# A fixed program order for ACT and DVE in the experts' blocks of a two-layer decoder trunk, with one call for a split ahead of every weight tile

## The chip, the cores and the metric

The kernel runs on one core of a Trainium2 chip. The metric is the time of one execution in device microseconds; lower is better. Engines are named as in the profile: PE does matrix products (PEld loads their stationary operand), ACT is ScalarE, DVE is VectorE, POOL is GpSimd, and SP here only issues DMAs.

## What is computed

Two decoder layers over 256 tokens of width 1024. Each has a mixer (four groups of heads), a feed-forward part and a gated per-layer embedding. The change touches the feed-forward part of the second layer only, which sends each token to two of eight experts:

```python
def moe_swiglu(x, router, w_gate, w_up, w_down):      # x: 256 x 1024, experts 1024 -> 3584 -> 1024
    logits = (x @ router).astype(jnp.float32)
    top_val, top_idx = lax.top_k(logits, TOP_K)        # 2 of 8
    top_w = jax.nn.softmax(top_val, axis=-1)
    combine = jnp.sum(jax.nn.one_hot(top_idx, N_EXPERTS, dtype=jnp.float32) * top_w[..., None], axis=-2)
    out = jnp.zeros_like(x)
    for e in range(N_EXPERTS):
        out = out + combine[..., e:e + 1].astype(x.dtype) * swiglu(x, w_gate[e], w_up[e], w_down[e])
    return out                                         # swiglu: (silu(x @ wg) * (x @ wu)) @ wd
```

All weights are float32.

## The kernel before

**Weights.** Every weight comes as a tile of 128 x 2048 float32 (1 MB). SP loads it into one of the `raw` buffers (seven in this part), in the order of a list (`plan`). For the matrix products a tile is cut into two parts: ACT copies it into `hi` in a rounded format (float32r), and DVE writes the rest, raw minus hi, into `lo`. There are five `hi` and five `lo` buffers in this part. `pop_split` does this, and `ready` is a list of tiles that were split early:

```python
    def ahead(n, parts=2, keep=False):
        ready.extend([pop_split(parts, keep) for _ in range(n)])
    ...
    def pop_split(parts=2, keep=False):
        if ready:
            return ready.pop(0)
        r = pop()
```

**Experts.** The eight experts are taken as four "large" ones (L, up to 128 tokens each) and four "small" ones (S, up to 64 tokens). Per expert, the hidden width of 3584 goes in seven blocks of 512. A block uses six tiles: two for the gate product (g1, g2), two for the up product (u1, u2) and two for the down product (d1, d2), 336 tiles in all. A large tile takes 12 products of 512 columns, a small one 8. `STEPS` pairs a block of a large expert with a block of a small one and puts the down products of the pair before behind them. A pair has twelve tiles, in this order: Lg1, Sg1, Lg2, (turn of the pair before), Sg2, Lu1, Su1, Lu2, Su2, Ld1, Sd1, Ld2, Sd2.

**Work between the tiles.** After Lg2 ACT takes silu of the gate product out of PSUM (`gate_up`, L1328). After Lu2 DVE multiplies it with the up product (L1331). After Sg2 and after Su2 ACT copies the small expert's products out. `turn` transposes the hidden block on PE: for the large expert 4 transposes, then a copy by ACT and a remainder by DVE; for the small one 8 products of 64 columns, silu by ACT (L1349), a product by DVE (L1350), and a split. After an expert's last block `scatter` copies the sums out of PSUM (two splits), multiplies them on PE with the selection, and adds them to `h` on DVE (L1383, four instructions). `gather` collects the tokens of the next two experts.

**What sets the order.** The framework's scheduler puts the instructions of each engine in an order of its own, as long as it respects the data; the order in which the code is written is only its input. On the chip each engine then takes its instructions in that order.

Of the kernel before, what the change touches and what calls it, by code (L numbers as in the profile page):

```python
# [3 lines left out]

# [1 line left out]

# [77 lines left out]
def decoder_trunk(ctx: ExitStack, tc: tile.TileContext, A, out):  # L84
# [27 lines left out]
    def T(tag, shape, dt=F32, keep=False):  # L112
        count[0] += 1
        name = f"{tag}_{count[0]}"
        if phase and tag + "+" in phase["bufs"] and not keep:
            n = BUFS[tag] + phase["bufs"][tag + "+"]
            turn[tag] = (turn.get(tag, -1) + 1) % n
            if turn[tag] >= BUFS[tag]:
                return phase["pool"].tile(shape, dt, name=name, tag=tag + "+", bufs=n - BUFS[tag])
        if tag in BUFS and (keep or not (phase and tag in phase["bufs"])):  # L120
            return sb.tile(shape, dt, name=name, tag=tag, bufs=BUFS[tag])
        return phase["pool"].tile(shape, dt, name=name, tag=tag, bufs=phase["bufs"][tag])

    def PS(tag, shape, dt=F32):
        count[0] += 1
        return ps.tile(shape, dt, name=f"p{tag}_{count[0]}", tag="p" + tag, bufs=BUFS[tag])

    V, S, G, PE = nc.vector, nc.scalar, nc.gpsimd, nc.tensor

    def f(ap):  # L130
        return ap.bitcast(F32)
# [66 lines left out]
    def split(x, o_hi, o_lo, note=True):  # L198
        a = act_copy(o_hi, x)
        b = V.tensor_tensor(o_lo, x, f(o_hi), op=ALU.subtract)  # L200
        if note:
            latest.update(act=a, dve=b)
        return a, b
# [4 lines left out]
    def ahead(n, parts=2, keep=False):  # L208
        ready.extend([pop_split(parts, keep) for _ in range(n)])
# [48 lines left out]
    def mm(o, l, r, start=True, stop=True):  # L258
        pe(PE.matmul(o, l, r, start=start, stop=stop, skip_group_check=True))  # L259
# [878 lines left out]
    def moe(cn, xh, xl):  # L1138
# [110 lines left out]
        def column(v, vx, kind, n, t):  # L1249
            r = rank_of(kind, n)  # L1250
            return v[:, t, 0:1] if (kind, n) == ("L", 0) else vx[:, t, r:r + 1]

        def gather(*places):

            s = T("S2", [P, 2, 256])
            width, at_ = 0, {}
            for kind, n in places:
                w = P if kind == "L" else 64
                at_[kind] = width
                for t in range(2):  # L1260
                    for c in range(2 if kind == "S" else 1):
                        V.tensor_scalar(s[:, t, width + c * w:width + c * w + w], iota[:, :w],
                                        column(pos, posx, kind, n, t), None, op0=ALU.is_equal)
                width += w
            if places[0] == ("L", 0):
                turned_slots(*places[0], s, 0)
            dst = {}
            for kind, n in places:
                if kind == "L":
                    gx = T("x", [P, 2, NK, P], F32R)  # L1270
                    dst[kind] = gx[:, 0], gx[:, 1]
                else:
                    gx = T("xs", [P, NK, P], F32R)
                    dst[kind] = gx[:, :, :64], gx[:, :, 64:]
                xg[kind, n] = gx
            k = 4 if width <= P else 2
            for q in range(NK // k):
                o = PS("e", [P, k, width])
                for c in range(k):
                    cc = slice((k * q + c) * P, (k * q + c + 1) * P)  # L1280
                    for t in range(2):
                        mm(o[:, c], cn[:, t, cc], s[:, t, :width], t == 0, t == 1)
                for kind, n in places:
                    w = P if kind == "L" else 64
                    split(o[:, :, at_[kind]:at_[kind] + w], *[v[:, k * q:k * q + k] for v in dst[kind]])
            for kind, n in places:
                if (kind, n) != ("L", 0):
                    turned_slots(kind, n, s, at_[kind])

        def turned_slots(kind, n, s, c0):  # L1290
            o = PS("e", [P, 2, P])
            for t in range(2):
                transpose(o[:, t, :], s[:, t, c0:c0 + P])
            st = T("S1", [P, 2, P], F32R)
            act_copy(st, o)
            sel[kind, n] = st
# [36 lines left out]
        def turn(u):  # L1333

            s = hid.pop(u)
            if u[0] == "L":
                pt = PS("e", [P, 4, P])
                for c in range(4):
                    transpose(pt[:, c, :], s[:, c * P:(c + 1) * P])
                hh, hl = T("S2", [P, 4, P], F32R), T("S2", [P, 4, P], F32R)  # L1340
                split(pt, hh, hl)
                hT[u] = hh, hl
            else:
                pt = PS("e", [P, 2, 4, 64])
                for g in range(2):
                    for c in range(4):
                        mm(pt[:, g, c, :], s[g][:, c * P:(c + 1) * P], cf[:, CF["halves"]])
                a = T("S1", [P, 4, 64])
                S.activation(a, pt[:, 0], AF.Silu)  # L1349
                V.tensor_tensor(a, a, pt[:, 1], op=ALU.mult)  # L1350
                hs = T("S2", [P, 4, P], F32R)
                split(a, hs[:, :, :64], hs[:, :, 64:])
                hT[u] = hs

        def down(u, q):
            p, b = u[:2], u[2]
# [14 lines left out]
        def scatter(p):  # L1371
            st = sel.pop(p)
            y = []
            for n in range(2):
                y.append((T("S2", [P, 512], F32R), T("S2", [P, 512], F32R)))
                split(acc[p][n], *y[n])
            for t in range(2):
                for n in range(2):
                    o = PS("e", [P, 512])
                    mm(o, st[:, t, :], y[n][0], True, False)  # L1380
                    mm(o, st[:, t, :], y[n][1], False, True)
                    hs = h[:, t, n * 512:(n + 1) * 512]
                    V.scalar_tensor_tensor(hs, o, column(comb, combx, *p, t), hs, op0=ALU.mult, op1=ALU.add)  # L1383

        full()
        gather(("L", 0))
        ahead(2, 4)
        hold()
        weights()
# [2 lines left out]
        chosen.extend(nc.values_load(order[0:1, r:r + 1], engines=[mybir.EngineType.SP], min_val=1, max_val=R)  # L1392
                      for r in range(R))
        follow(S.preload_act_table_set("silu_and_others"), fence["act"])
        ahead(2)
        for u, t in STEPS:
            if t is None:
                for v in u:
                    turn(v)
                done = dict(latest)  # L1400
            elif t < 4:
                gate_up(u, t)
            else:
                down(u, t - 4)
            if (u, t) == (("L", 0, 0), 3):
                gather(("S", 0))
            if t == 5 and u[0] == "L" and u[2] == 4 and u[1] < 3:
                gather(("L", u[1] + 1), ("S", u[1] + 1))
        fence.update(done)

    def spill(cn, pos, comb, capacities, over):
# [223 lines left out]
```

## Time and profile before

| | us |
|---|---|
| median of 3 runs (1661.75 to 1662.02) | 1661.79 |
| the profiled execution | 1662.77 |
| its span, first to last instruction | 1661.0 |

| busy, share | PE | PEld | DVE | ACT | POOL |
|---|---|---|---|---|---|
| whole span | 95% | 80% | 78% | 65% | 5% |
| 710 to 1605 us | 97% | 77% | 90% | 76% | 0% |

The experts' blocks fill the second row's stretch and a little on either side: the first gate product leaves PSUM at 690.86 us. "Busy" of PE is a modelled figure: in a row of matmuls that follow each other without a gap, each is listed with 390 to 400 ns and starts 0.23 us after the one before. What PE was idle for, and whom it waited for, says more than its share. A releaser that the profile names ("<-") is the one that came last.

### The profile page before, as it was taken

Reading aid. Unit: us, or ns where it says so; the run is one execution under the profiler, and the core shown is the slowest. Engines: PE = TensorE matmul, PEld = TensorE weight load, DVE = VectorE, ACT = ScalarE, POOL = GpSimd, SP = SyncE. Lnnn points to the kernel's source line nnn. Section 1 sums busy time; section 2 is a strip of 40 time slices with the busy share of each in tenths; the row PEclk is TensorE's granted clock in tenths of the full one; section 3 lists DMA queues with packets and bytes.
Section 4 is the critical chain, followed back from the end, with each engine's and each line's share of the span. In section 5 each row is a group of like instructions: output and inputs, shape, how many; then the busy total and the mean of one; then the engine's idle time right before and its main releaser. Section 6 shows DMA issues by size and latency. Waiting matters only on the chain.

```text
span 1661.0 us, 22588 instructions
## 1 busy us (share of the span) xinstructions
PE 1582.1 (95%) x8523; PEld 1321.2 (80%) x8523; DVE 1302.6 (78%) x1470; ACT 1073.6 (65%) x1315; POOL 80.2 (5%) x116
## 2 busy tenths in 40 slices
PE   7998999999999998799999999999999999999998
PEld 7897789999888977677787777787777787777776
DVE  5578655455575786788988998898998989989895
ACT  5555554444455563677777777777687777777773
POOL 0024100000000141000000000000000000000000
PEclk9998999999999999899999999999999999999999
DMA  8431465545444222499999999999999999999990
GB/s 324 173 107 57 161 233 176 205 157 210 143 159 183 97 98 77 166 420 386 385 365 397 372 355 398 403 371 370 355 380 386 388 373 362 371 385 388 399 348 26
DMA packets 65489, 461.26 MB, mean 278 GB/s; under 512 B 7392, under 2 KB 7776, under 8 KB 12128
## 3 DMA queue, kind: packets, MB, share of 16 engines
q1 hardware_dynamic: 64224, 455.02, 71.6%
q10 hardware_dynamic: 1152, 4.76, 0.9%
q8 instruction: 68, 1.11, 0.3%
q14 instruction: 45, 0.37, 0.1%
HBM read 458.70 MB, written 1.05 MB: 277 GB/s over the span
## 4 chain that ended last, share of the span: by engine, by line
PE 32%; DVE 12%; ACT 6%; issue 5%; DMA 3%; ACTq 0%; DVEq 0%; POOLq 0%; POOL 0%
DVE lo L200 10%; ACT hi L134 5%; PE pc L255 5%; PE pc L256 4%; PE pc L1305 4%; PE pc L254 4%; PE pc L1306 4%; PE pe L259 4%; PE pd L255 2%; PE pd L256 2%; PE pd L254 2%; DMA raw<-in_moe_dn_dram 2%; DMA raw<-in_moe_gu_dram 1%; PE pe L271 1%; ACT S L134 1%
## 5 line engine op out<-in xcount | busy, mean ns | idle before, releaser
L200 DVE TENSOR_TENSOR lo<-raw,hi 128x2048 fp32r<-128x2048 f32 (+4 forms) x532 | 958.3, 1844 | 183.3 <-ACT hi L134 182.7
L134 ACT ACTIVATE hi<-raw 128x2048 fp32r<-128x2048 f32 (+4 forms) x532 | 796.4, 1556 | 118.8 <-PE pc L256 84.3
L255 PE MATMUL pc<-lo,x 128*128 128x512 f32 x512 | 207.5, 405 | 16.4 <-DVE lo L200 15.8
L254 PE MATMUL pc<-hi,x 128*128 128x512 f32 x512 | 204.0, 399 | 3.2 <-DVE rank L1233 2.1
L256 PE MATMUL pc<-hi,x 128*128 128x512 f32 x512 | 202.8, 396 | 0.0
L1306 PE MATMUL pc<-lo,xs 128*128 128x512 f32 x448 | 178.7, 399 | 7.6 <-DVE lo L200 7.4
L254 PE MATMUL pd<-x,hi 128*128 128x256 f32 x640 | 181.7, 284 | 0.1
L256 PE MATMUL pd<-x,lo 128*128 128x256 f32 x640 | 181.5, 284 | 0.0
L255 PE MATMUL pd<-x,hi 128*128 128x256 f32 x640 | 180.7, 283 | 0.3 <-DVE x L200 0.3
L1305 PE MATMUL pc<-hi,xs 128*128 128x512 f32 x448 | 177.0, 395 | 1.3 <-DVE S L1331 0.9
L255 PEld LDWEIGHTS pc<-lo,x 128*128 128x128 f32 x512 | 96.5, 188 | 55.8 <-DVE lo L200 35.7
L254 PEld LDWEIGHTS pd<-x,hi 128*128 128x128 f32 x640 | 121.6, 190 | 1.6 <-ACT x L134 0.3
L256 PEld LDWEIGHTS pd<-x,lo 128*128 128x128 f32 x640 | 121.6, 190 | 1.6 <-DVE lo L200 0.2
L255 PEld LDWEIGHTS pd<-x,hi 128*128 128x128 f32 x640 | 121.6, 190 | 1.2 <-DVE x L200 0.5
L254 PEld LDWEIGHTS pc<-hi,x 128*128 128x128 f32 x512 | 96.7, 189 | 25.9 <-issue 2.2
L256 PEld LDWEIGHTS pc<-hi,x 128*128 128x128 f32 x512 | 96.7, 189 | 20.7 <-DVE x L200 0.4
L1306 PEld LDWEIGHTS pc<-lo,xs 128*128 128x128 f32 x448 | 84.2, 188 | 34.9 <-DVE lo L200 17.4
L1305 PEld LDWEIGHTS pc<-hi,xs 128*128 128x128 f32 x448 | 84.1, 188 | 21.3 <-DVE S L1331 1.8
L255 PE MATMUL pd<-lo,S 128*128 128x512 f32 x224 | 91.1, 407 | 5.4 <-DVE lo L200 5.4
L256 PE MATMUL pd<-hi,S 128*128 128x512 f32 x224 | 88.3, 394 | 0.0
L1306 PE MATMUL pc<-lo,S 128*128 128x512 f32 x224 | 82.7, 410 | 0.8 <-DVE lo L200 0.8
L254 PE MATMUL pd<-hi,S 128*128 128x512 f32 x224 | 79.4, 395 | 0.0
(278 smaller groups left out, 2290.7 us busy)
## 6 DMA issues: line engine op xcount, KB each, us to landing
raw<-in_moe_gu_dram SPq DMA_DIRECT2D x224, 1024.0 KB, 7.2
raw<-in_moe_dn_dram SPq DMA_DIRECT2D x112, 1024.0 KB, 7.5
raw<-in_ffn_gu_dram SPq DMA_DIRECT2D x28, 1024.0 KB, 5.0
raw<-in_ffn_dn_dram SPq DMA_DIRECT2D x14, 1024.0 KB, 4.9
raw<-in_win_t_dram SPq DMA_DIRECT2D x16, 848.0 KB, 5.2
raw<-in_win_c_dram SPq DMA_DIRECT2D x12, 1024.0 KB, 6.8
raw<-in_cmp_w_dram SPq DMA_DIRECT2D x8, 1024.0 KB, 5.9
raw<-in_w_out_dram SPq DMA_DIRECT2D x8, 1024.0 KB, 4.9
```

The lines of the kernel that those rows point to most:

```text
L134: return S.activation(o, i, AF.Copy, scale=scale)
L200: b = V.tensor_tensor(o_lo, x, f(o_hi), op=ALU.subtract)
L254: pe(PE.matmul(o, lh, rh, start=start, stop=False))
L255: pe(PE.matmul(o, lh, rl, start=False, stop=False))
L256: pe(PE.matmul(o, ll, rh, start=False, stop=stop))
L259: pe(PE.matmul(o, l, r, start=start, stop=stop, skip_group_check=True))
L271: pe(PE.transpose(o, i, ident[:i.shape[0], :i.shape[0]]))
L1305: pe(PE.matmul(o, lhs, rh, start=start, stop=False))
L1306: pe(PE.matmul(o, lhs, rl, start=False, stop=stop))
```

## The change

ACT and DVE get a wrapper (`Engine`). While `keep(True)` holds, each instruction that goes through it is tied to the one issued before it on the same engine, by an ordering dependency that costs no semaphore: the scheduler can no longer move them against each other. PE, SP and POOL are left to the scheduler. Since every call then passes through the wrapper, all of ACT's and DVE's instructions in these blocks carry its line number, L146.

The loop over `STEPS` calls `ahead(1, 1)` before each tile's products. Ahead of the loop, `ahead(2)` becomes `gather(("S", 0))` and `ahead(1)`. Parts of `gather` (four products each with their copies, and the turned selections), the last two steps of the small expert's `turn`, and the four parts of `scatter` are put into a list `later`; one entry of it is issued after each tile's products.

```diff
+    class Engine:
+        def __init__(self, eng):
+            self.eng, self.kept, self.last = eng, False, None
+        def keep(self, on):
+            self.kept, self.last = on, None
+        def __getattr__(self, name):
+            op = getattr(self.eng, name)
+            if not self.kept:
+                return op
+            def given(*args, **kw):
+                ins = op(*args, **kw)
+                if self.last:
+                    follow(ins, self.last)
+                self.last = ins
+                return ins
+            return given
+
+    V, S = Engine(nc.vector), Engine(nc.scalar)
...
-            for q in range(NK // k):
+            def part(q):
                 o = PS("e", [P, k, width])
...
+            for q in range(NK // k):
+                later.append(partial(part, q))
             for kind, n in places:
                 if (kind, n) != ("L", 0):
-                    turned_slots(kind, n, s, at_[kind])
+                    later.append(partial(turned_slots, kind, n, s, at_[kind]))
...
+            def times():
                 V.tensor_tensor(a, a, pt[:, 1], op=ALU.mult)
+            def parts():
                 hs = T("S2", [P, 4, P], F32R)
                 split(a, hs[:, :, :64], hs[:, :, 64:])
                 hT[u] = hs
+            later[:0] = [times, parts]
...
+            later.extend(partial(part, t, n) for t in range(2) for n in range(2))
+        def some(n=None):
+            while later and n != 0:
+                later.pop(0)()
+                n = n and n - 1
...
         ahead(2, 4)
...
-        ahead(2)
+        gather(("S", 0))
+        ahead(1)
+        V.keep(True)
+        S.keep(True)
         for u, t in STEPS:
             if t is None:
                 for v in u:
                     turn(v)
                 done = dict(latest)
-            elif t < 4:
+                continue
+            ahead(1, 1)
+            if t < 4:
                 gate_up(u, t)
             else:
                 down(u, t - 4)
-            if (u, t) == (("L", 0, 0), 3):
-                gather(("S", 0))
+            some(1)
...
+        V.keep(False)
+        S.keep(False)
+        some()
```

The lists below are the built programs' order, engine by engine. In them `hi_1761_9498` is a weight tile's hi part (the numbers tell tiles apart), `pc_...` is a product in PSUM that comes from the tiles named beside it, `pe_...` a small product in PSUM, `S1_...` and `S2_...` are results in SBUF. All are of one pair in the second large expert.

ACT before, from the split of tile Lg2 (`hi_1762`) on; the gate product of Lg1 and Lg2 is `pc_1753`, that of Sg1 and Sg2 (`hi_1772`) is `pc_1757`:

```order
L134 ACTIVATE hi_1762_9502<-raw_1736_9396 128x2048
L134 ACTIVATE hi_1772_9546<-raw_1739_9410 128x2048
L134 ACTIVATE hi_1777_9563<-raw_1742_9428 128x2048
L1328 ACTIVATE S2_1764_9518<-pc_1753_9466 128x512
L134 ACTIVATE S2_1766_9525<-pe_1765_9520 128x512
L134 ACTIVATE hi_1781_9582<-raw_1754_9467 128x2048
L134 ACTIVATE hi_1784_9596<-raw_1758_9486 128x2048
L134 ACTIVATE hi_1787_9615<-raw_1761_9500 128x2048
L1349 ACTIVATE S1_1769_9538<-pe_1768_9529 128x256
L134 ACTIVATE hi_1791_9631<-raw_1771_9544 128x2048
L134 ACTIVATE S2_1770_9541<-S1_1769_9538 128x4x64
L134 ACTIVATE S2_1774_9558<-pc_1757_9485 128x512
```

ACT after the change, from the split of the same tile (Lg2 is `hi_1761` here, Sg2 `hi_1771`, Lu1 `hi_1775`, Su1 `hi_1780`, Lu2 `hi_1784`, Su2 `hi_1787`, Ld1 `hi_1791`):

```order
L146 ACTIVATE hi_1761_9498<-raw_1736_9396 128x2048
L146 ACTIVATE S2_1763_9514<-pc_1753_9460 128x512
L146 ACTIVATE S2_1766_9525<-pe_1765_9520 128x512
L146 ACTIVATE S1_1769_9538<-pe_1768_9529 128x256
L146 ACTIVATE hi_1771_9542<-raw_1739_9410 128x2048
L146 ACTIVATE S2_1773_9554<-pc_1758_9483 128x512
L146 ACTIVATE hi_1775_9559<-raw_1742_9428 128x2048
L146 ACTIVATE S2_1778_9576<-S1_1769_9538 128x4x64
L146 ACTIVATE hi_1780_9581<-raw_1750_9454 128x2048
L146 ACTIVATE hi_1784_9596<-raw_1755_9477 128x2048
L146 ACTIVATE hi_1787_9615<-raw_1760_9496 128x2048
L146 ACTIVATE S2_1789_9627<-pc_1782_9585 128x512
```

The copies out of PSUM (`<-pc`) stood two to five splits behind the split of the tile that completes the product; now each stands directly behind that split, ahead of the next tile's.

DVE before, the same pair, from the remainder of Sg2 (`lo_9547`) to that of Ld1 (`lo_9632`); L1331 is the large expert's product of gate and up:

```order
L200 TENSOR_TENSOR lo_9547<-raw_9410,hi_9546 128x2048
L200 TENSOR_TENSOR lo_9564<-raw_9428,hi_9563 128x2048
L1383 SCALAR_TENSOR_TENSOR h<-pe_9462,combx,h 128x512
L200 TENSOR_TENSOR S_1767_9526<-pe_9520,S_1766_9525 128x512
L200 TENSOR_TENSOR lo_9583<-raw_9467,hi_9582 128x2048
L200 TENSOR_TENSOR lo_9597<-raw_9486,hi_9596 128x2048
L200 TENSOR_TENSOR lo_9616<-raw_9500,hi_9615 128x2048
L1350 TENSOR_TENSOR S_1769_9538<-S_1769_9538,pe_9529 128x256
L1331 TENSOR_TENSOR S_1764_9518<-S_1764_9518,pc_9560 128x512
L200 TENSOR_TENSOR lo_9632<-raw_9544,hi_9631 128x2048
```

DVE after the change, from the remainder of Sg2 (`lo_9543`) to that of Ld1 (`lo_9632`):

```order
L146 TENSOR_TENSOR lo_9543<-raw_9410,hi_9542 128x2048
L146 TENSOR_TENSOR S_1769_9538<-S_1769_9538,pe_9529 128x256
L146 TENSOR_TENSOR lo_9560<-raw_9428,hi_9559 128x2048
L146 TENSOR_TENSOR S_1778_9576<-S_1769_9538,S_1778_9576 128x4x64
L146 TENSOR_TENSOR lo_9582<-raw_9454,hi_9581 128x2048
L146 TENSOR_TENSOR lo_9597<-raw_9477,hi_9596 128x2048
L146 TENSOR_TENSOR S_1763_9514<-S_1763_9514,pc_9563 128x512
L146 TENSOR_TENSOR lo_9616<-raw_9496,hi_9615 128x2048
L146 TENSOR_TENSOR lo_9632<-raw_9540,hi_9631 128x2048
```

The product with `pc_9563`, which needs all of Lu1's and Lu2's matmuls, moved ahead of the remainder of Su2 (`lo_9616`).

## Rows read from the trace of the kernel before

**Rows 1.** The page's span, and busy us (share) xinstructions by engine

```profile
span 1661.0 us, 22588 instructions
PE 1582.1 (95%) x8523; PEld 1321.2 (80%) x8523; DVE 1302.6 (78%) x1470; ACT 1073.6 (65%) x1315; POOL 80.2 (5%) x116
```

**Rows 2.** Busy time by stretch: from:to, us, PE PEld DVE ACT POOL, PEclk, DMA, GB/s

```profile
710.00:1605.00 895.00, 863.85 (x3948) 685.69 (x3947) 807.27 (x511) 679.59 (x531) 0.00 (x0) 1.00 0.98 381
```

**Rows 3.** Waits, 710 to 1605 us: who waits for whom, us in total, times, longest

```profile
ACT S L1328 <- PE pc L256: 75.6, 26, 4.1
...
PE pc L255 <- DVE lo L200: 15.8, 38, 0.9
```

**Rows 4.** Waits of SP's DMA queue, 710 to 1605 us, same columns

```profile
SPq L186 <- DVE lo L200: 560.9, 268, 5.3
```

**Rows 5.** Groups by line and shape, 700 to 1610 us: busy us, mean ns | idle before

```profile
L200 DVE TENSOR_TENSOR lo<-raw,hi 128x2048 fp32r<-128x2048 f32 x329 | 738.3, 2286 | 61.7 <-ACT hi L134 61.7
L1331 DVE TENSOR_TENSOR S<-S,pc 128x512 f32<-128x512 f32 x28 | 19.2, 687 | 19.1 <-PE pc L256 19.1
...
L1383 DVE SCALAR_TENSOR_TENSOR h<-pe,combx,h 128x512 f32<-128x512 f32 x20 | 14.4, 743 | 0.0
L200 DVE TENSOR_TENSOR S<-S,S 128x256 fp32r<-128x256 f32 x28 | 11.7, 418 | 0.0
...
L200 DVE TENSOR_TENSOR x<-pe,x 128x256 fp32r<-128x256 f32 x12 | 4.8, 417 | 1.9 <-ACT x L134 1.9
...
L134 ACT ACTIVATE hi<-raw 128x2048 fp32r<-128x2048 f32 x329 | 610.3, 1912 | 0.0
L134 ACT ACTIVATE S<-pc 128x512 f32<-128x512 f32 x56 | 33.3, 595 | 36.8 <-PE pc L1306 36.6
...
L1349 ACT ACTIVATE S<-pe 128x256 f32<-128x256 f32 x28 | 10.8, 384 | 55.2 <-PE pe L259 55.2
```

**Rows 6.** ACT in order of time: start us, us, what [idle before <-releaser]

```profile
708.06 0.60 ACT L1328 ACTIVATE S<-pc 128x512 f32<-128x512 f32 x1 [3.41 <-PE pc L256]
...
735.45 0.60 ACT L1328 ACTIVATE S<-pc 128x512 f32<-128x512 f32 x1 [2.19 <-PE pc L256]
...
739.00 7.34 ACT L134 ACTIVATE hi<-raw 128x2048 fp32r<-128x2048 f32 x4
...
767.66 0.60 ACT L1328 ACTIVATE S<-pc 128x512 f32<-128x512 f32 x1 [3.03 <-PE pc L256]
...
1566.47 0.60 ACT L1328 ACTIVATE S<-pc 128x512 f32<-128x512 f32 x1 [3.09 <-PE pc L256]
```

**Rows 7.** DVE in order of time, same columns: six remainders in a row

```profile
755.64 13.30 DVE L200 TENSOR_TENSOR lo<-raw,hi 128x2048 fp32r<-128x2048 f32 x6 [1.38 <-ACT hi L134]
```

**Rows 8.** PE's matmuls in order of time, then ACT's copy of their product

```profile
911.64 0.39 PE L1305 MATMUL pc<-hi,xs 128*128 128x512 f32 x1
911.87 0.39 PE L1306 MATMUL pc<-lo,xs 128*128 128x512 f32 x1
...
912.30 0.60 ACT L134 ACTIVATE S<-pc 128x512 f32<-128x512 f32 x1 [1.63 <-PE pc L1306]
```

**Rows 9.** The chain that ended last: half a small expert's turn on PE

```profile
724.78 0.84 PE pe L259 x8
```

**Rows 10.** Busy time by stretch, columns as in rows 2: PE's clock falls

```profile
149.00:158.00 9.00, 8.53 (x25) 5.85 (x26) 7.47 (x24) 4.72 (x15) 3.03 (x4) 0.50 0.35 117
...
662.00:668.00 6.00, 2.83 (x15) 1.90 (x15) 5.24 (x9) 2.47 (x6) 0.75 (x2) 0.92 0.00 0
668.00:673.00 5.00, 4.44 (x22) 2.83 (x20) 3.79 (x6) 3.27 (x6) 0.00 (x0) 0.50 0.30 105
...
1630.00:1636.00 6.00, 5.55 (x15) 4.44 (x16) 6.00 (x7) 5.82 (x7) 0.00 (x0) 0.50 0.02 4
```

**Rows 11.** PE's matmuls in order of time in the last of these stretches

```profile
1632.22 0.63 PE L255 MATMUL pc<-lo,x 128*128 128x512 f32 x1
1632.64 0.63 PE L256 MATMUL pc<-hi,x 128*128 128x512 f32 x1
```

More of the change, by code (lines that the diff above doesn't have):

```diff
@@ L3 @@
 from contextlib import ExitStack, contextmanager
+from functools import partial
 import numpy as np
@@ L126, in PS @@
         return ps.tile(shape, dt, name=f"p{tag}_{count[0]}", tag="p" + tag, bufs=BUFS[tag])
-    V, S, G, PE = nc.vector, nc.scalar, nc.gpsimd, nc.tensor
+    G, PE = nc.gpsimd, nc.tensor
+    class Engine:
[15 more added lines that the diff above has]
+    V, S = Engine(nc.vector), Engine(nc.scalar)
     def f(ap):
@@ L1285, in gather @@
                     split(o[:, :, at_[kind]:at_[kind] + w], *[v[:, k * q:k * q + k] for v in dst[kind]])
+            for q in range(NK // k):
+                later.append(partial(part, q))
             for kind, n in places:
                 if (kind, n) != ("L", 0):
-                    turned_slots(kind, n, s, at_[kind])
+                    later.append(partial(turned_slots, kind, n, s, at_[kind]))
+        later = []
         def turned_slots(kind, n, s, c0):
@@ L1342, in turn @@
                 hT[u] = hh, hl
[L1343 to L1349, printed above, removed]
+                return
+            pt = PS("e", [P, 2, 4, 64])
+            for g in range(2):
+                for c in range(4):
+                    mm(pt[:, g, c, :], s[g][:, c * P:(c + 1) * P], cf[:, CF["halves"]])
+            a = T("S1", [P, 4, 64])
+            S.activation(a, pt[:, 0], AF.Silu)
+            def times():
                 V.tensor_tensor(a, a, pt[:, 1], op=ALU.mult)
+            def parts():
                 hs = T("S2", [P, 4, P], F32R)
@@ L1376, in scatter, with part @@
                 split(acc[p][n], *y[n])
[L1377 to L1383, printed above, removed]
+            def part(t, n):
+                o = PS("e", [P, 512])
+                mm(o, st[:, t, :], y[n][0], True, False)
+                mm(o, st[:, t, :], y[n][1], False, True)
+                hs = h[:, t, n * 512:(n + 1) * 512]
+                V.scalar_tensor_tensor(hs, o, column(comb, combx, *p, t), hs, op0=ALU.mult, op1=ALU.add)
+            later.extend(partial(part, t, n) for t in range(2) for n in range(2))
[3 more added lines that the diff above has]
+                n = n and n - 1
         full()
         gather(("L", 0))
+        some()
         ahead(2, 4)
@@ L1404, in moe @@
                 down(u, t - 4)
-            if (u, t) == (("L", 0, 0), 3):
-                gather(("S", 0))
+            some(1)
             if t == 5 and u[0] == "L" and u[2] == 4 and u[1] < 3:
                 gather(("L", u[1] + 1), ("S", u[1] + 1))
+        V.keep(False)
+        S.keep(False)
+        some()
         fence.update(done)
```

## The prediction, made before the changed kernel ran

> **What bounds the kernel now.** On the page PE is busy 95% of the span and DVE 78% [rows 1], an average over stages, so I read the table by stretch next, then the waits there, then the groups by line, then two engines in order of time. In the experts' part PE is busy 863.85 of 895 us at the full clock [rows 2], so 31.2 us of idle time is all that a better order of the splits can win. PE waits, when it does, for `lo`, the last step of a split [rows 3]. ACT waits much longer for PE: 75.6 us in 26 waits before silu of the gate product alone [rows 3]. That costs nothing, because ACT has by then split the tiles that PE needs next: the copy stands two to five splits behind its tile in the order printed above. DVE is the next engine: 807 of 895 us [rows 2], 738.3 us of its time being remainders [rows 5]. SP issues its loads when DVE has freed a raw buffer [rows 4], so transfers follow DVE and set nothing. A pair of twelve tiles takes 767.66 - 735.45 = 32.21 us where no gather or scatter falls in it, and (1566.47 - 708.06) / 26 = 33.02 us in the mean of 26 [rows 6].
>
> **What the change does to the lead.** `pop_split` hands out from `ready` as long as something is in it. When the loop starts, `ready` holds two tiles; `ahead(1)` takes the first and puts it back at the end, the first `ahead(1, 1)` turns the list back, and two products later it is empty. From the third tile on, `ahead(1, 1)` splits the very tile whose products follow. So in program order a split stands directly ahead of its own products, behind everything that the tile before gave to ACT and DVE, and the wrapper makes that order binding. The order lists show it: ACT's copy of `pc_1753`, which needs all of Lg2, stands before the split of Sg2. The lead is four only where no copy comes between (Ld1 to Lg2); at four places of each pair it is none, and PE has to stop.
>
> **The price of the four stops.** Prices: split on ACT 1.91, remainder on DVE 2.29, copy 0.60, small silu 0.38, product 0.69, small remainder 0.42 [rows 5]; remainders in a row every 13.30 / 6 = 2.22 [rows 7]; a matmul every 0.23 [rows 8]. From the time at which PE could start its next matmul to ACT's start on the product it is 912.30 - 911.87 - 0.23 = 0.20 [rows 8]; ACT starts 0.04 after the matmul's end there, and I take 0.04 for the handovers from ACT to DVE and from DVE to PE too. A pair is a chain, each stop beginning at the end of PE's work on a tile:
>
> A, after Lg2: PE does the small expert's turn, 2 x 0.84 [rows 9]; 0.20; silu 0.38; split of Sg2 1.91; 0.04; remainder 2.29; 0.04; seven of Sg2's eight matmuls 1.61. The two copies ahead of that silu lie beside the turn. Sum 8.15.
>
> B, after Sg2: 0.20 + copy 0.60 + split of Lu1 1.91 + 0.04 + remainder 2.29, then DVE's small remainder 0.42 and the remainders of Su1 and Lu2, 2 x 2.22, then 0.04 and eleven of Lu2's twelve matmuls 2.53. Sum 12.47. PE's work on Lu1 and Su1 lies beside the remainders.
>
> C, after Lu2: 0.20 + DVE's product 0.69 + remainder of Su2 2.22 + 0.04 + 1.61. Sum 4.76.
>
> D, after Su2: 0.20 + copy 0.60 + split of Ld1 1.91 + 0.04 + remainder 2.29, then six remainders without a stop, 6 x 2.22 = 13.32, then 0.04 + 2.53 to the end of the next Lg2. Sum 20.93. In this stretch PE's tiles (2.76 and 1.84 us, mean 2.3) just keep up with DVE.
>
> A pair takes 46.31 us, 14.10 more than now; 336 tiles are 28 pairs: +395 us.
>
> **Scatter and gather.** A scatter puts two copies between two splits. After a large expert's last tile the distance from one remainder's end to the next becomes 0.04 + ten matmuls 2.30 + 0.20 + 0.60 + a second copy 0.50 (ACT's instructions in a row overlap: four splits take 7.34 [rows 6]) + 1.91 + 0.04 + 2.29 = 7.88 in place of 2.22, so +5.7; after a small one's, with six matmuls, +4.7. Its `h` updates, eight a place at 0.74 [rows 5] less 0.09 of overlap, go between remainders in stretch D, where DVE is the chain: +5.2. Four places: 4 x 15.6 = 62. A gather gives DVE four pieces of at least 0.42 [rows 5], and each of its four copies on ACT may hold the next split up; I bound it by 2 and by 21 us (four stops of 4.7, as after a scatter, on top of that) and take 7, near DVE's own work because two pieces wait while a stop is on anyway. Three gathers: 21. Of these 83 us the kernel before already pays (33.02 - 32.21) x 26 = 21. Net +62, between 27 (gathers at 2, `h` updates hidden: 42 + 6 - 21) and 104 (gathers at 21: 62 + 63 - 21). This deals out the pieces one a tile but takes none away; that edit by itself I cost at nothing, since the pieces stand behind a stop that is there with or without them.
>
> PE's instructions stay the same; SP's loads come later but the ring still holds seven tiles, and the DMA share of 0.98 falls with the rate. No price from SP.
>
> **PE's clock.** All of the experts' part ran at 1.00 before [rows 2]. [...] In stops A and B together PE does two tiles' worth of work in some 13 us, and in D's first 5 us it does less than 2 us; both are emptier than the gap at 662. I take two falls a pair at 2.0 each (the gap that they are nearest to), 28 x 4.0 = +112; the ends are 0 and 28 x 7.8 = 218.
>
> [...]
>
> **The sum.** The profiled execution took 1662.77 us, 0.98 more than the median, so I count from the median: 1662 + 395 + 62 + 112 = **2231 us**.
>
> **Rivals.**
> 1. The clock stays up: everything as above without the 112. 1662 + 457 = 2119, from 2084 (27 for scatter and gather) to 2161 (104). For it: the experts' part never left 1.00 so far. Against it: the fall behind 662, after a milder gap.
> 2. The clock stays down through the whole part. With 0.43 for 0.23, A is 3.1 + 4.9 + 3.0 = 11.0, B 5.1 + thirty matmuls 12.9 = 18.0, C 3.2 + 3.0 = 6.2, D 5.1 + seventy matmuls 30.1 = 35.2; a pair 70.4, 38.2 more than now, so 1662 + 28 x 38.2 + 62 = 2794. Against it: stretch D has some 16 us of nearly unbroken matmuls, and no low stretch of rows 10 was longer than 9.
> 3. The split really runs four tiles ahead of PE, as the change's name has it. Then every copy on ACT falls while four tiles are ready, PE's idle time goes, and the time is 1662 - 31 = 1631, the only way to faster. It decides itself by the list: with four tiles in `ready` at the loop's start it would hold. Against it: the order of ACT printed above.
> 4. The binding order costs and saves nothing because the queues between the engines even it out: 1662. Against it: the order lists differ, and an instruction that waits on ACT holds the split behind it.
>
> **How the numbers follow.** The stops are read off an order that is built, so cases with them hold nearly everything: my forecast 0.68 (2165 to 2340), rival 1 0.22, rival 2 or a clock that is down most of the time 0.05, rival 3 0.03, rival 4 0.02. The range takes in the forecast's own and most of rival 1: 2095 to 2335. Faster by over 0.2% (about what a measurement can tell from no change) 0.03, within 0.2% 0.02, slower 0.95.
>
> **What would show it.** In the profile after, ACT's and DVE's work of this part stands at L146. Right: a plain pair (silu to silu of the gate product) near 50 us, 46 without the clock; PE idle some 16 us a pair, about half of it before the first matmul on a new `hi` (waiting for ACT) and half before the first on a new `lo`; the longest waits of ACT on `pc`, now with PE idle behind them; the granted clock of the stage between 0.75 and 0.9; the DMA share near 0.65. Wrong: a pair of 32 us or less, or no matmul waiting for ACT's `hi` (then the lead is there); PE's idle time as priced but the clock at 1.00 (rival 1); a stage clock under 0.6 (rival 2). If PE waits for raw tiles to land, the free SP queue was a mistake.

## The result and the profile after

The changed kernel takes 2264.65 us (median of 4 runs, 2262.07 to 2266.58) against 1661.77 us for the kernel before beside it: a ratio of 1.3627, with a 95% interval of 1.3603 to 1.365. The profiled execution took 2262.89 us, its span 2261.1. Nearly all of the difference of 603 us lies in the experts' blocks.

From the page after, the span and the granted clock in 40 slices:

```profile
span 2261.1 us, 22581 instructions
...
PEclk9999999999998887787887887888888788887788
```

The table by stretch, for the experts' part of after (from, to, length, then busy time and instructions of PE, PEld, DVE, ACT and POOL, then granted clock, DMA share, GB/s):

```profile
710.00:2205.00 1495.00, 1100.33 (x3996) 815.83 (x3996) 824.70 (x518) 685.21 (x536) 0.00 (x0) 0.81 0.61 230
```

ACT and DVE do the work that they did in [rows 2], in a stretch that is 600 us longer. PE is idle for 394.7 us of it where it was idle for 31.2, and its clock is 0.81 in place of 1.00.

ACT's longest waits in the same stretch (engine, tile and line, whom it waited for, then total, times, longest); everything that ACT and DVE do here stands at L146, the wrapper's line, and PE's lines have moved (L280 to L282 are a large expert's products, L1337 and L1338 a small one's):

```profile
ACT S L146 <- PE pc L1338: 483.1, 59, 13.2
...
ACT S L146 <- PE pc L282: 233.5, 26, 10.1
```

Before, the largest total was 75.6 us [rows 3], and PE had work beside it. Now these waits are followed by waits of PE, as the groups by line show (busy and mean ns, then the idle time ahead of the group and what ended it):

```profile
L146 DVE TENSOR_TENSOR lo<-raw,hi 128x2048 fp32r<-128x2048 f32 x329 | 739.3, 2286 | 337.4 <-ACT hi L146 337.4
L146 ACT ACTIVATE hi<-raw 128x2048 fp32r<-128x2048 f32 x326 | 603.0, 1904 | 3.0 <-PE pd L282 3.0
L1337 PE MATMUL pc<-hi,xs 128*128 128x512 f32 x447 | 214.8, 481 | 119.9 <-ACT hi L146 119.9
L1338 PE MATMUL pc<-lo,xs 128*128 128x512 f32 x448 | 213.0, 475 | 89.1 <-DVE lo L146 89.1
L280 PE MATMUL pc<-hi,x 128*128 128x512 f32 x431 | 193.7, 449 | 69.2 <-ACT hi L146 68.8
...
L280 PE MATMUL pd<-hi,S 128*128 128x512 f32 x223 | 101.5, 498 | 37.1 <-ACT hi L146 37.1
...
L1337 PE MATMUL pc<-hi,S 128*128 128x512 f32 x212 | 91.1, 475 | 27.2 <-ACT hi L146 27.2
```

A split takes as long as before (1904 and 2286 ns beside the 1912 and 2286 of [rows 5]): no split has become slower, each comes later. PE waits 119.9 + 68.8 + 37.1 + 27.2 = 253.0 us for `hi`, and 89.1 for the small expert's `lo`.

One plain pair in order of time shows the loop that closes. ACT's copies out of PSUM (start, duration, in square brackets the idle time ahead and its releaser):

```profile
818.13 0.60 ACT L146 ACTIVATE S<-pc 128x512 f32<-128x512 f32 x1 [9.87 <-PE pc L282]
...
819.37 1.92 ACT L146 ACTIVATE hi<-raw 128x2048 fp32r<-128x2048 f32 x1
827.06 0.60 ACT L146 ACTIVATE S<-pc 128x512 f32<-128x512 f32 x1 [5.77 <-PE pc L1338]
...
845.91 0.60 ACT L146 ACTIVATE S<-pc 128x512 f32<-128x512 f32 x1 [10.74 <-PE pc L1338]
...
869.28 0.60 ACT L146 ACTIVATE S<-pc 128x512 f32<-128x512 f32 x1 [9.86 <-PE pc L282]
```

And PE between them:

```profile
817.70 0.40 PE L282 MATMUL pc<-hi,x 128*128 128x512 f32 x1
821.34 0.50 PE L1337 MATMUL pc<-hi,xs 128*128 128x512 f32 x1 [3.24 <-ACT hi L146]
823.67 0.79 PE L1338 MATMUL pc<-lo,xs 128*128 128x512 f32 x1 [1.83 <-DVE lo L146]
...
829.51 0.80 PE L280 MATMUL pc<-hi,x 128*128 128x512 f32 x1 [2.48 <-ACT hi L146]
831.61 0.80 PE L1337 MATMUL pc<-hi,xs 128*128 128x512 f32 x1 [1.31 <-ACT hi L146]
```

At 818.13 ACT takes Lg2's product, for which it has waited 9.87 us; only then, at 819.37, does it split Sg2, which is the next thing PE needs, and PE stands from 818.1 to 821.34. The same comes back at 827.06, 845.91 and 869.28. The pair takes 869.28 - 818.13 = 51.15 us; before it took 32.21 [rows 6]. The plain pairs of this trace (those without a gather, a scatter or a neighbour of one) take 51.05 to 51.25.

### The profile page after: what moved, and what is told of

It is laid out like the page before. It is cut to its first block, busy times and chain, and to the rows that moved or that the text cites. A ratio compares the mean times of both kernels' runs of the same rounds, so it can differ in the third digit from the quotient of the medians.

```text
span 2261.1 us, 22581 instructions
## 1 busy us (share of the span) xinstructions
PE 1809.5 (80%) x8523; PEld 1442.7 (64%) x8523; DVE 1309.3 (58%) x1470; ACT 1073.0 (47%) x1315; POOL 80.2 (4%) x116
## 3 DMA queue, kind: packets, MB, share of 16 engines
q10 hardware_dynamic: 1152, 4.76, 0.6%
## 5 line engine op out<-in xcount | busy, mean ns | idle before, releaser
L146 DVE TENSOR_TENSOR lo<-raw,hi 128x2048 fp32r<-128x2048 f32 x334 | 750.7, 2286 | 339.3 <-ACT hi L146 339.3
L146 ACT ACTIVATE hi<-raw 128x2048 fp32r<-128x2048 f32 x334 | 617.7, 1904 | 3.0 <-PE pd L282 3.0
L146 ACT ACTIVATE S<-pc 128x512 f32<-128x512 f32 (+1 forms) x92 | 54.9, 597 | 733.5 <-PE pc L1338 484.5
L1337 PE MATMUL pc<-hi,xs 128*128 128x512 f32 x448 | 215.2, 480 | 119.9 <-ACT hi L146 119.9
L280 PE MATMUL pc<-hi,x 128*128 128x512 f32 x512 | 227.3, 444 | 74.2 <-ACT hi L146 70.9
L1338 PE MATMUL pc<-lo,xs 128*128 128x512 f32 x448 | 213.0, 475 | 89.1 <-DVE lo L146 89.1
L226 DVE TENSOR_TENSOR lo<-raw,hi 128x1024 fp32r<-128x1024 f32 (+4 forms) x198 | 208.7, 1098 | 120.8 <-ACT hi L160 120.4
L281 PE MATMUL pc<-lo,x 128*128 128x512 f32 x512 | 224.1, 438 | 14.3 <-DVE lo L146 13.8
L160 ACT ACTIVATE hi<-raw 128x1024 fp32r<-128x1024 f32 (+4 forms) x198 | 176.7, 955 | 119.6 <-PE pc L282 84.3
L282 PE MATMUL pc<-hi,x 128*128 128x512 f32 x512 | 219.4, 429 | 0.0
L1337 PEld LDWEIGHTS pc<-hi,xs 128*128 128x128 f32 x448 | 100.8, 225 | 162.6 <-ACT hi L146 144.9
L280 PEld LDWEIGHTS pc<-hi,x 128*128 128x128 f32 x512 | 110.4, 216 | 120.7 <-ACT hi L146 92.0
L1338 PEld LDWEIGHTS pc<-lo,xs 128*128 128x128 f32 x448 | 100.3, 224 | 129.3 <-DVE lo L146 107.2
L280 PE MATMUL pd<-x,hi 128*128 128x256 f32 x640 | 182.4, 285 | 0.1
L282 PE MATMUL pd<-x,lo 128*128 128x256 f32 x640 | 182.1, 285 | 0.0
L281 PEld LDWEIGHTS pc<-lo,x 128*128 128x128 f32 x512 | 107.7, 210 | 43.5 <-DVE lo L146 20.1
L280 PE MATMUL pd<-hi,S 128*128 128x512 f32 x224 | 101.9, 497 | 37.1 <-ACT hi L146 37.1
L282 PEld LDWEIGHTS pc<-hi,x 128*128 128x128 f32 x512 | 108.6, 212 | 25.9 <-DVE x L226 0.4
L280 PEld LDWEIGHTS pd<-x,hi 128*128 128x128 f32 x640 | 122.4, 191 | 1.6 <-ACT x L160 0.3
L282 PEld LDWEIGHTS pd<-x,lo 128*128 128x128 f32 x640 | 122.2, 191 | 1.5 <-DVE lo L226 0.2
```

Source lines behind the costliest of these rows:

```text
L146: ins = op(*args, **kw)
L160: return S.activation(o, i, AF.Copy, scale=scale)
L280: pe(PE.matmul(o, lh, rh, start=start, stop=False))
L281: pe(PE.matmul(o, lh, rl, start=False, stop=False))
L282: pe(PE.matmul(o, ll, rh, start=False, stop=stop))
L1337: pe(PE.matmul(o, lhs, rh, start=start, stop=False))
```

## Experiments

Two theories stood against each other at first: that the loss comes from the split standing directly ahead of its own products (a lead of none), and that it comes from a bound order as such.

### The binding: none, ACT's alone, DVE's alone

Three kernels keep the changed code and take away calls of the wrapper's switch. `free`:

```diff
-        V.keep(True)
-        S.keep(True)
...
-        V.keep(False)
-        S.keep(False)
```

> The changed kernel without the binding: the scheduler may move ACT's and DVE's instructions again; the loop, the list and the pieces dealt out stay. The lists of ACT show the copies one to three splits behind their tiles again. Theory (binding without a lead makes the stops): 1655 to 1675 us, as before the change. Rival (dealing out the pieces costs): above 1700 us.

Measured: 1660.68 us (10 runs), ratio 0.9984, interval 0.9974 to 0.9993. Calls for a split ahead of every tile, the pieces dealt one a tile and the gather that is placed earlier cost nothing as long as the scheduler sets the order: in its own order two splits, at a few places three, stand between a tile's split and the copy of its product, whatever the code says. Without the binding there is no loss at all.

`act_only` drops the two lines on V, `dve_only` the two on S; each was run once.

> Only ACT bound to program order, DVE left to the scheduler. Theory: stops A, B and D are ACT's (a copy ahead of the next split) and stay; stop C, DVE's product ahead of the remainder of Su2, goes, 28 x 1.5 to 3.5 us: 2165 to 2225 us. Rival (DVE's order is the larger part): below 2000 us.

Measured: 2148.88 us, 16 below the range. A plain pair takes 806.72 - 758.73 = 47.99 us:

```profile
758.73 0.60 ACT L146 ACTIVATE S<-pc 128x512 f32<-128x512 f32 x1 [7.96 <-PE pc L282]
767.65 0.60 ACT L146 ACTIVATE S<-pc 128x512 f32<-128x512 f32 x1 [5.77 <-PE pc L1338]
784.38 0.60 ACT L146 ACTIVATE S<-pc 128x512 f32<-128x512 f32 x1 [8.63 <-PE pc L1338]
806.72 0.60 ACT L146 ACTIVATE S<-pc 128x512 f32<-128x512 f32 x1 [9.12 <-PE pc L282]
```

The stops behind ACT's three copies are still there, so ACT's order by itself brings 486 of the 603 us.

> Only DVE bound to program order, ACT left to the scheduler. Theory: only stop C stays, some 3 to 5 us a pair, with the clock mostly at 1.00: 1740 to 1810 us. Rival (DVE's order is the larger part): above 1950 us.

Measured: 1902.54 us, between the two theories. Stop C alone does not explain it: by the waits there (710 to 1700 us), DVE's bound order has a second cost, which I had not counted. The remainder of each turn reads a copy that ACT, now free, makes when it likes, and the next `lo` is held behind it:

```profile
DVE S L146 <- ACT S L160: 180.9, 52, 6.2
...
PE pc L1338 <- DVE lo L146: 98.5, 54, 3.9
DVE S L146 <- PE pc L282: 80.1, 24, 5.4
```

486 and 240 us add up to more than 603; that the two orders hold partly the same stops would explain it, but no run here shows it.

### The lead: one, two and four splits, with the order still bound

The list `ready` gets a helper that adds to its end instead of turning it round; the three kernels differ in how many tiles it holds before the loop (`left` counts the tiles still to be split). With four:

```diff
+    def more(n, parts=2):
+        held, ready[:] = ready[:], []
+        ready.extend(held + [pop_split(parts) for _ in range(n)])
...
-        ahead(1)
+        more(2)
...
-            ahead(1, 1)
+            if left[0]:
+                more(1, 1)
+                left[0] -= 1
```

`lead2` leaves `more(2)` out, `lead1` splits only while `ready` holds fewer than two.

> The change with a real lead: before the loop the list of split tiles is filled to four, and each step appends one freshly split tile, so that every copy out of PSUM stands four splits behind its tile on ACT; ACT and DVE stay bound to program order. Theory (the four stops of a pair come from the missing lead): the stops go, a pair takes 31 to 32 us, the time is 1630 to 1650 us, the clock of the part stays at 1.00. Rival (a bound order costs whatever the lead, since one instruction that waits holds all behind it): above 1750 us. Rival (the pieces dealt out one a tile cost): above 1700 us.

> The changed kernel with one split, not none, standing ahead of the tile whose products come next. Theory (the four stops a pair come from the split standing directly before its own tile's products): a lead of one tile lets the split of the next tile run while the copy out of PSUM still waits, so the stops shrink to what a silu or a turn adds to one tile's 4.2 us of VectorE work; plain pair 37 to 41 us against 51.2, program 1830 to 1950 us. Rival (the bound order itself costs the time, whatever the lead): pair 47 us or more, program above 2100 us.

> The changed kernel with two splits, not none, standing ahead of the tile whose products come next: about the lead that the kernel before has at its PSUM copies, with the program's order kept on ACT and DVE. Theory (the lead alone makes the time in plain pairs; the bound order costs only where pieces of gather and scatter stand): plain pair 30 to 32.5 us, pairs with pieces 36 to 39 us, program 1690 to 1750 us, between 1829 at a lead of one and 1701 at four. Rival (a bound order needs no more lead than the order before had, and pieces cost nothing at this lead): program 1640 to 1670 us.

Measured, with a plain pair and the fifth to ninth pair (those in which the gather for the second experts, the scatter of the first and their neighbours fall), both read from the starts of silu of the gate product in order of time:

| splits ahead | program, us | plain pair | five pairs with pieces | these, less five plain |
|---|---|---|---|---|
| 0 (changed kernel) | 2264.65 | 51.15 | 286.7 | 31 |
| 1 (one run) | 1829.48 | 36.23 | 205.2 | 24 |
| 2 | 1724.71 | 31.70 | 190.3 | 32 |
| 4 | 1700.60 | 29.81 | 188.8 | 40 |
| kernel before, unbound | 1661.77 | 32.21 | 168.7 | 8 |

(Ratios: 1.0367 with an interval of 1.035 to 1.0384 at two, 1.0232 with 1.0215 to 1.0249 at four.) The first theory holds for the plain pairs: one split of lead takes 15 of the 19 us back (`lead1` came out just below both of its ranges), two bring the pair below the kernel before, four make it 2.40 us shorter. The second theory keeps a part of the truth: the kernel before has at least the lead of `lead2`, but unbound, and its five pairs take 168.7 us where the bound ones take 190.3. The rows for one and two, three pairs each, are 855.22 - 746.52 and 833.01 - 737.90 (`lead1`, then `lead2`):

```profile
746.52 0.60 ACT L146 ACTIVATE S<-pc 128x512 f32<-128x512 f32 x1 [5.35 <-PE pc L286]
...
855.22 0.60 ACT L146 ACTIVATE S<-pc 128x512 f32<-128x512 f32 x1 [5.63 <-PE pc L286]
```

```profile
737.90 0.60 ACT L146 ACTIVATE S<-pc 128x512 f32<-128x512 f32 x1 [5.50 <-PE pc L286]
...
833.01 0.60 ACT L146 ACTIVATE S<-pc 128x512 f32<-128x512 f32 x1 [5.52 <-PE pc L286]
```

My expected 1630 to 1650 us for a lead of four missed, by the pairs with pieces: their clock was not at 1.00 but at 0.94 (824.39 to 1013.20 us), and the 1700.60 us stand at the bound of the theory that the pieces cost. In `lead4` ACT waits for PE's small products, and DVE for those of the scatter (710 to 1600 us):

```profile
ACT S L146 <- PE pe L301: 56.6, 9, 9.9
ACT S L146 <- PE pe L289: 42.8, 11, 7.1
ACT x L146 <- PE pe L289: 25.0, 3, 9.2
...
DVE h L146 <- PE pe L289: 21.5, 6, 5.3
```

The last two are the pieces' own: the gather's copies and the scatter's sums. Most of the first two belongs to the turns, by the groups by line: 53.6 us to the large expert's copy and 36.9 to the small one's silu, which are also issued in the step of their matmuls. The large expert's copy:

```profile
L146 ACT ACTIVATE S<-pe 128x512 fp32r<-128x512 f32 x26 | 15.5, 594 | 53.6 <-PE pe L301 53.6
```

In the plain pairs looked at (734.5 to 794.39 and 1013.20 to 1043.01 us) ACT has no wait on `pe`. In order of time, the first copy of the first gather:

```profile
854.02 0.38 ACT L146 ACTIVATE x<-pe 128x256 fp32r<-128x256 f32 x1 [7.07 <-PE pe L289]
```

When ACT runs four tiles ahead, PE is four tiles behind: a copy of a piece that was issued in the same step waits until PE has come up to its matmuls, 7.07 us here, and the lead is gone. From a lead of one on, the pieces cost more the further ahead the splits stand, 24, 32 and 40 us per five pairs; the copies' waits as the reason are tested by `spaced` below.

### The clock

`filler` is the changed kernel with products whose result nobody reads, which keep PE busy in three of the four stops:

```diff
+        def fill(n):
+            e = PS("e", [P, 512])
+            line.append(spare["p"])
+            for _ in range(n):
+                mm(e, spare["l"], spare["r"])
+            line.clear()
...
+            if u[0] == "S":
+                fill((10, 6)[g])
...
+                if (u and spare) and u[0][0] == "L" and t is None:
+                    fill(10)
```

> The changed kernel with throw-away products (10 of 128x512 behind the turn, 10 behind the small expert's gate, 6 behind its up) that keep TensorE busy in three of the four stops; nothing of the computation is left out. Theory (some 4 to 5 us of each pair's 51.2 are matmuls at the lower clock after a stop): the granted clock of the experts' stretch stays at 0.97 to 1.00 against 0.81, a plain pair takes 46 to 48 us, the program 2110 to 2170 us. Rival (the clock's fall is hidden in the stops, where TensorE waits anyway): clock up as well, pair 50 to 52 us, program 2230 to 2290 us.

Measured: 2172.76 us (one run), 2.8 us above the range, with the clock of the stretch at 0.93 where 0.97 to 1.00 was expected: more work on PE, and 92 us less time. So a part of the loss is the clock. The table by stretch cuts a plain pair of after into five pieces, and one of `filler` into three (columns as above):

```profile
818.13:822.00 3.87, 0.50 (x1) 0.19 (x1) 1.37 (x2) 3.15 (x4) 0.00 (x0) 0.96 0.32 133
822.00:835.00 13.00, 7.53 (x16) 5.15 (x17) 7.46 (x6) 7.94 (x6) 0.00 (x0) 0.50 0.38 133
835.00:849.00 14.00, 11.13 (x54) 8.37 (x53) 5.07 (x4) 3.26 (x4) 0.00 (x0) 0.99 0.64 251
849.00:855.50 6.50, 5.43 (x14) 4.19 (x14) 6.50 (x4) 6.50 (x4) 0.00 (x0) 0.50 0.61 212
855.50:869.28 13.78, 13.74 (x59) 10.79 (x57) 8.34 (x4) 3.74 (x4) 0.00 (x0) 0.99 1.00 394
```

```profile
814.54:836.50 21.96, 15.32 (x61) 11.14 (x61) 12.45 (x9) 11.28 (x10) 0.00 (x0) 1.00 0.66 250
836.50:843.50 7.00, 6.16 (x16) 4.81 (x17) 1.12 (x2) 2.77 (x3) 0.00 (x0) 0.51 0.42 153
843.50:862.33 18.83, 18.79 (x91) 15.27 (x89) 15.17 (x7) 10.46 (x7) 0.00 (x0) 1.00 0.84 322
```

In after the clock is at 0.50 twice a pair, from stop A through most of B and again at D's start, with 7.53 + 5.43 = 12.96 us of busy time. In the first of these stretches 512-column matmuls in a row start 0.43 us apart (at 832.63, 833.06 and 833.49), where at 1.00 they start 0.23 apart [rows 8]; from these two numbers I estimate 46% of the busy time as lost, 6.0 us. In `filler` one low stretch is left, at 0.51, 6.16 us busy, by the same share 2.8 us lost, and the pair takes 47.79. Both come to the same pair without the clock: 51.15 - 6.0 = 45.2 and 47.79 - 2.8 = 45.0 us. This last step is an estimate, since some of the slow matmuls lie beside DVE's remainders.

### The pieces of gather and scatter

`undealt` is the changed kernel with `some()` in place of `some(1)`: all pieces at once.

> The changed kernel with all pieces of a gather or scatter, and the small turn's two late operations, issued at once in the step that makes them instead of one a tile. Theory (at a lead of zero TensorE stands right in front of each piece, so that dealing hides nothing and each piece costs its own hand-overs): within 40 us of the changed kernel, 2225 to 2305 us, plain pair 50 to 53 us. Rival (dealing is itself a cause of the loss, by putting a piece's hand-overs ahead of each split): below 2200 us; (dealing saves): above 2320 us.

Measured: 2265.08 us (one run), the changed kernel's time; a plain pair still takes 51.2. Dealing the pieces out is worth nothing at a lead of none, and costs nothing.

With a lead of four the question was how to have pieces without their waits. `lead4_free` is `lead4` without the binding. `lead4_plain` binds the order only while no more than two pieces are left:

```diff
+            plain = len(later) <= 2
+            if plain != V.kept:
+                V.keep(plain)
+                S.keep(plain)
```

> The version with splits really four tiles ahead, with ACT and DVE left to the scheduler's order instead of the program's. Theory (a true lead of four takes 2.4 us out of a plain pair, and the bound order costs it back where pieces of a gather or scatter stand): without the bound order both hold or neither, 1625 to 1650 us. Rival (the scheduler goes by its own priorities and the lead falls back to about two): 1655 to 1670 us, the time of the kernel before.

> The version with splits really four tiles ahead, with ACT and DVE bound to the program's order only in the steps where no piece of a gather or scatter is left to issue. Theory (the bound order costs its 40 to 70 us only in the pairs with pieces): plain pairs 29.8 us, pairs with pieces near the 33.6 of the kernel before, 1620 to 1650 us. Rival (the loss sits where the order is bound, in all pairs alike): 1680 us or more.

Measured: 1660.39 us for `lead4_free` (ratio 0.9985, interval 0.9975 to 0.9994). The rival was right: the scheduler goes back to its two splits, and the lead written into the code is gone. `lead4_plain`: 1670.18 us (1.0048, 1.0032 to 1.0065), between the two theories. The five pairs come from 188.8 to 175.2 us, not to the kernel before's 168.7. What holds them there is not shown: ACT, where it is bound, still waits 43.5 us for the small turn's silu and other copies of `pe`, but `spaced_cut` below has more of such waits and is faster.

`spaced` keeps the binding throughout and takes the wait's reason away: a piece's matmuls are issued in one step, its copies (for a scatter its sums into `h`) three steps later.

```diff
+                def copies():
+                    for kind, n in places:
+                        w = P if kind == "L" else 64
+                        split(o[:, :, at_[kind]:at_[kind] + w], *[v[:, k * q:k * q + k] for v in dst[kind]])
+
+                return copies
...
+            copied(i)
...
-            some(1)
+            if soon:
+                soon.pop(0)()
+            if later and not owed and all(v is not None for _, v in STEPS[i + 1:i + 4]):
+                owed.append((i + 3, later.pop(0)()))
```

> Splits four tiles ahead, order bound, and each piece of a gather or scatter cut in two: its matmuls are issued in one step, its copies out of PSUM three steps later, never across a turn; the first gather is issued whole ahead of the blocks. Theory (with a lead of four, a piece's copy makes ACT and DVE wait until TensorE has come up to it, and this is what the pieces' pairs cost): ACT's waits for the pieces' matmuls fall from 120 us to under 40, pairs with pieces come from 37.9 to 31 to 34 us, plain pairs stay at 29.8, program 1600 to 1650 us. Rival (the pieces' own work, or the copies of the accumulators at the scatter, is what costs): pairs with pieces stay above 35 us, program above 1670 us.

Measured: 1642.84 us, ratio 0.9877, interval 0.986 to 0.9893, 1.2% less than the kernel before. The five pairs take 165.6 us. The waits of the pieces themselves have nearly gone (ACT's `x` from 25.0 to 4.9 us, DVE's `h` from 21.5 to 5.2), and with them the large turn's (from 53.6 to none). But ACT's waits on `pe` as a whole came from 124 to 66 us, not under 40 as expected, and of the 57.0 in the first row 52.3 are the small turn's silu. A second wait shows:

```profile
ACT S L146 <- PE pe L289: 57.0, 14, 6.4
ACT xs L146 <- DVE x L146: 33.1, 12, 3.2
```

The second is a piece whose two copies (`x` for the large expert, `xs` for the small one) read one PSUM tile. ACT's read of it waits until DVE has read it (12 waits, 3.2 us at most), although neither writes there, and in the wait below, of 2.43 us, DVE has a remainder (873.78 to 876.07 us) to finish first:

```profile
873.65 0.36 ACT L146 ACTIVATE x<-pe 128x256 fp32r<-128x256 f32 x1
876.44 0.28 ACT L146 ACTIVATE xs<-pe 128x128 fp32r<-128x128 f32 x1 [2.43 <-DVE x L146]
```

Why one read waits for the other is not shown by these runs. `spaced_cut` tests whether it is a matter of their order: it issues both copies of ACT ahead of both subtractions of DVE:

```diff
-                        split(o[:, :, at_[kind]:at_[kind] + w], *[v[:, k * q:k * q + k] for v in dst[kind]])
+                        cut.append((o[:, :, at_[kind]:at_[kind] + w], *[v[:, k * q:k * q + k] for v in dst[kind]]))
+                    for x, hi, _ in cut:
+                        latest["act"] = act_copy(hi, x)
+                    for x, hi, lo in cut:
+                        latest["dve"] = V.tensor_tensor(lo, x, f(hi), op=ALU.subtract)
```

> The version with spaced pieces, and in each gather piece both copies of ACT issued ahead of both subtractions of DVE. Theory (in the version before, the small expert's copy on ACT stands behind DVE's subtraction of the large expert's part of the same PSUM tile, 33 us in 12 waits, and ACT's next splits behind that): these waits are gone, pairs in which a gather runs fall from 33 to 39.6 us towards 31 to 34 us, program 1612 to 1638 us. Rival (these waits lie in ACT's slack beside the weights' transfers, whose share is 0.98): 1639 to 1650 us.

Measured: 1629.69 us, ratio 0.9796, interval 0.978 to 0.9813. The same place in order of time:

```profile
874.34 0.36 ACT L146 ACTIVATE x<-pe 128x256 fp32r<-128x256 f32 x1
874.60 0.26 ACT L146 ACTIVATE xs<-pe 128x128 fp32r<-128x128 f32 x1
```

ACT's waits of `xs` on DVE, 33.1 us in `spaced`, are not in the list of `spaced_cut` any more (710 to 1570 us). The five pairs take 160.8 us. The small turn's silu still waits (in all, then behind a gather's first piece):

```profile
ACT S L146 <- PE pe L289: 68.1, 17, 7.4
```

```profile
865.54 0.38 ACT L146 ACTIVATE S<-pe 128x256 f32<-128x256 f32 x1 [7.19 <-PE pe L289]
```

That pair takes 36.6 us, where 31 to 34 were expected. The sum of such waits is no price by itself: it is larger here than in `spaced`, and before the same silu waited 55.2 us [rows 5]. The change's idea thus works when the lead is really four and the pieces' copies stand well behind their matmuls in the bound order: 34 us less than the kernel before.

## Why the prediction was right, and where its terms were off

2231 us were predicted, in a range of 2095 to 2335; 2264.65 came.

**The lead.** Right, and the runs show it: the loss needs the binding (`free`) and a lead of none (`lead1` to `lead4`). Rival 3 asked what four splits in `ready` would do. Filling the list to four would not have been enough, since `ahead` takes from that same list; `lead4` needed `more`. Without most of the pieces' waits (`spaced_cut`) it comes to 1629.69, where the rival said 1631. The agreement is luck. I took PE's 31.2 idle us [rows 2] as all that there is to win, and that is wrong: a plain pair of `lead4` is 2.40 us shorter, 28 such would be 67 us, and the pairs with pieces give part of that back. A plain pair before and one in `lead4`, in the table by stretch:

```profile
735.45:767.66 32.21, 31.02 (x141) 24.41 (x140) 28.75 (x17) 24.50 (x19) 0.00 (x0) 1.00 1.00 393
```

```profile
1013.20:1043.01 29.81, 29.81 (x140) 24.54 (x139) 28.63 (x18) 24.86 (x18) 0.00 (x0) 1.00 1.01 422
```

The same work, at the same clock, is 31.02 us busy in the one and 29.81 in the other. In the pair before PE waits three times for a `lo`, 0.43, 0.46 and 0.30 us as listed. The first of them:

```profile
739.89 0.40 PE L1305 MATMUL pc<-hi,xs 128*128 128x512 f32 x1
740.72 0.50 PE L1306 MATMUL pc<-lo,xs 128*128 128x512 f32 x1 [0.43 <-DVE lo L200]
```

The two start 0.83 us apart, where in a row it is 0.23, so 0.60 is lost there and only 0.43 listed as idle; the rest goes into busy time. By their starts (0.83, 0.86 and 0.70 us) the three waits cost 1.70 us of the 2.40. A share of 97% hid time that could be won.

**The four stops.** All are there, at the places given. From the end of PE's work on one tile to the next they measure 8.9, 14.0, 4.9 and 23.4 us where 8.15, 12.47, 4.76 and 20.93 were priced without the clock. The chain was priced 1.2 us too dear (46.31 against the 45.0 to 45.2 above): in A it counted the small turn, 2 x 0.84 [rows 9], which PE does earlier, in the gaps of C and D.

**The clock.** Two falls a pair, as forecast, to 0.50; rival 1 (no fall) is out by the clock of 0.81. The term is mis-sized: some 6.0 us of matmul time are lost a pair, by the estimate above, not 4.0. The 2.0 us a fall, and the 3.9 of the upper end, were my estimate, 46% of the 4.44 and 8.53 us that PE was busy at 0.50 in 668 to 673 us (behind the gap at 662, 2.83 us busy of 6) and in 149 to 158 us [rows 10], by matmuls every 0.43 us (0.42 in [rows 11]) for 0.23. No run shows 2.0 us as the price of a fall in the experts' part; the runs showed 7.53 and 5.43 us busy at 0.50 in a pair, and the first low stretch is 13 us long, longer than any in [rows 10]. Rival 2 (low throughout) is out as well: the clock comes back to 0.99 twice a pair, for 14.0 and 13.8 us, the third and the fifth stretch above. In this pair it falls the first time behind PE's wait of 3.24 us ahead of 821.34, the second time behind 840.60 to 849.00 us, where PE was busy 5.53 us of 8.40.

**Sum of a pair.** 1.2 too much and 2.0 too little: 46.31 + 4.0 = 50.31 against 51.15. Times 28, that is 23.5 of the 34 us by which the forecast was low.

**Scatter and gather.** What the plain pairs leave is 603 - 28 x (51.15 - 32.21) = 73 us against 62; 11 too little, inside its bounds of 27 and 104. Dealing the pieces was costed at nothing, and `undealt` agrees.

**What would show it.** The pair (51.15), the clock (0.81) and the DMA share (0.61 for 0.65) came as said, and PE does not wait for raw tiles. PE's idle time was said to be some 16 us a pair, half before `hi` and half before `lo`. It is 394.7 us in 1495, or 14.3 in a mean pair of (2132.22 - 720.47) / 26 = 54.3, and not in halves: 253.0 us stand before `hi`, 89.1 before the small expert's `lo`. In stops B and D PE takes the first product of the next tile before the remainder is ready, and waits for that tile's `hi` instead (the 1.31 us at 831.61).

## What to carry to other kernels

An order that is bound on engines which take their work in turn is only as good as the distance in it between a producer and its consumer: count, in the order as built, how many splits stand between a tile and the copy of its product, and don't trust the number in the code (a list whose filling call takes from the list itself had a lead of none). A plain pair took 51.15 us here at a distance of none and 29.81 at four. Once the lead is there, anything put into the bound order that waits for the engine which runs behind can cost that lead (a piece's copy waited 7.07 us in `lead4`); issue its matmuls early and its copies some steps later (three, at a lead of four, here). Where a busy share is near 100%, compare the same work in two traces before taking the idle rest for all that can be won (31.02 and 29.81 us busy here, where 1.19 and none were idle).

## What the hardware showed that was not expected

The DMA share said little about the rate here: it reads 1.00 at 393 GB/s in a plain pair before and 1.01 at 422 in `lead4`, in the rows above. Twelve tiles of 1.049 MB in 29.81 us are 422 GB/s, and in two other plain pairs of `lead4` (734.5 to 794.39 us) ACT's splits begin to wait for transfers:

```profile
ACT hi L146 <- DMA raw<-in_moe_gu_dram: 6.2, 11, 0.7
```

PE has no idle time in these pairs (29.81 us busy of 29.81 in the row above, 30.00 of 30.00 in 740 to 770 us), so it bounds them, at 29.8 to 30.0 us, and by these waits, 0.7 us at most, the transfers are close behind. How much above 422 GB/s they could go is not shown.
